# Recurrent stage of a two-block transformer: gates and gelu branch multiplied as plain fp32, statistics' matmuls placed later in three fillers

## The chip, the cores and the metric

The kernel runs on one core of a Trainium2 chip. The metric is the device time of one execution in microseconds (us). The engines are named as in the profile: PE is the matrix engine (PEld its weight loads), DVE the vector engine, ACT the scalar engine, POOL the general-purpose engine, SP the engine whose queue issues the weight transfers.

## What is computed

Two transformer blocks, one after the other, on 256 tokens of 1024 features, all in float32. The first block is, per layer, a gated feed-forward network (FFN), a mixing stage and a second FFN, each followed by a residual and a layer norm; the mixing stage of layer 0 is the recurrent one that the change is about, that of layer 1 is a dilated attention.

```python
def rglru_block(x, w_in, conv_w, conv_b, gate_w, gate_b, lam, w_out):
    y_br, u_br = jnp.split(x @ w_in, 2, axis=-1)          # 1024 -> 2 x 1280
    y = jax.nn.gelu(y_br)
    u = causal_depthwise_conv(u_br, conv_w, conv_b)
    h = rg_lru(u, gate_w, gate_b, lam)
    return (y * h.astype(y.dtype)) @ w_out                # 1280 -> 1024

def rg_lru(u, gate_w, gate_b, lam):
...
    gates = jnp.einsum("bsnc,gncd->gbsnd", ublk, gate_w.astype(jnp.float32)).reshape(2, bsz, s, r)   # 5 blocks of 256 x 256
    gates = gates + gate_b.astype(jnp.float32)[:, None, None, :]
    rec_gate = jax.nn.sigmoid(gates[0])
    in_gate = jax.nn.sigmoid(gates[1])
    log_a = -LRU_C * rec_gate * jax.nn.softplus(-lam.astype(jnp.float32))
    a = jnp.exp(log_a)
    b = jnp.sqrt(-jnp.expm1(2.0 * log_a)) * (in_gate * uf)
...
    _, h = lax.associative_scan(combine, (a, b), axis=1)  # h[t] = a[t] h[t-1] + b[t]
    return h
```

The second block puts 16 more tokens in front (272 in all), norms them, and has two layers of a hybrid mixer and an FFN.

## The kernel before

**Weights.** All weights lie in memory as a stream of 537 units, in the order in which they are used. A unit is eight tiles of 128x128 floats, 512 KB. `_dma` issues the transfer of a unit to one of five `raw` buffers (`RAWS`) on SP's queue. A product of two floats is made of three matmuls of a shorter float format (`F32R`): ACT rounds the weights to `whi` (`_hi`, L88, two casts of 128x512 a unit), DVE subtracts to get the rest `wlo` (`_lo`, L100, two subtractions a unit), and `mm3` multiplies whi by the high part of the data, whi by the low part, wlo by the high part. The data are split in the same way: `gh`, `gl` for a norm's output, `uch`, `ucl` for the convolution's, `yh`, `yl` for the recurrent stage's result, `hh`, `hl` for an FFN's middle. Seven buffers each hold whi and wlo; `pump` keeps them up to six units ahead of use (`LOOK`). With `lo_pool` set, as it is from the end of the recurrent stage's filler to its output projection, `_lo` puts the subtraction on POOL.

**A stage.** `out_proj` ends each stage: per output block of 128 features it sums on PE, then DVE adds the residual (L253), ACT squares (L199), ACT and DVE scale and split the not yet normed data into gh and gl, and running sums of x and of x squared over the blocks go to `acc` (`sums`, L194 and L195, on POOL mostly; the last block's on DVE, L229 and L230). A plain fp32 matmul with a tile of ones (`stats`) adds acc over the partitions and gives the norm's mean and variance. While that is under way, PE does the next stage's `filler`: 32 tiles on the not yet normed data, whose result is corrected afterwards (`fix`). `norm` then writes the normed `xf`, gh and gl. `when` says behind which of the filler's tiles `stats` is called; it is called under a priority raised by 100, and a scheduler sorts each engine's instructions by priority.

**The recurrent stage** (`rg`), from unit 66: filler (4 units), `Pu` (4 units), then, in the order in which PE runs them after the change, gates(0), `Pu2` (units 75 and 76), gates(1), gates(2), gelu(0), gates(3), gelu(1), gates(4), gelu(2), gelu(3), gelu(4). `conv(n)` is eight DVE instructions on a 128x256 half each (L509, L511) that make `uc`, and a split of uc. `gates(n)` is one unit, eight tiles. `gelu(n)` is two units, sixteen tiles on gh and gl, then gelu on ACT and DVE. `root`, `scan` and `close` make the recurrence (the scan is L562) and the split result yh, yl (L160 on ACT, L161 on DVE). out_proj takes units 91 to 100; its first wave sums four output blocks together, k = 0 to 9 in order, half a unit for each k, and needs yh and yl of close(2) at k = 4, of close(4) at k = 8.

Of the kernel before, what the change touches and what calls it, by code (L numbers as in the profile page):

```python
# [8 lines left out]
F32 = mybir.dt.float32  # L9
# [5 lines left out]
SEQ = 256  # L15
# [7 lines left out]
NLN = 11  # L23
LN_EMB = 6
ALPHA = 2.0 ** 0.5
EPS = 1e-5
# [10 lines left out]
KVB = 5  # L37
RAWS = 5
N_HEADS = 16
SLOPES = [2.0 ** (-8.0 * (h + 1) / N_HEADS) for h in range(N_HEADS)]  # L40
# [18 lines left out]
class Builder:  # L59
# [21 lines left out]
    def _hi(self):  # L81
        u = self.nhi
        while self.ndma < min(u + RAWS, N_UNIT):
            self._dma()
        self.nhi += 1
        hi = self.p_w.tile([128, UNIT * 128], F32R, tag="whi", name="whi")
        for q in range(0, UNIT * 128, 512):
            self.nc.scalar.copy(hi[:, q:q + 512], self.raws[u][:, q:q + 512])  # L88
        self.his[u] = hi

    def _lo(self, pool=False):
        u = self.nlo
        while self.nhi <= u:
            self._hi()
        self.nlo += 1
        lo = self.p_w.tile([128, UNIT * 128], F32R, tag="wlo", name="wlo")
        eng = self.nc.gpsimd if pool or self.lo_pool else self.nc.vector
        r, h = self.raws.pop(u), self.his[u].bitcast(F32)
        for q in range(0, UNIT * 128, 512):
            eng.tensor_tensor(lo[:, q:q + 512], r[:, q:q + 512], h[:, q:q + 512], op=ALU.subtract)  # L100
        self.los[u] = lo
# [10 lines left out]
    def w(self, spec, n=1):  # L112
        t = self.used
        u, o = divmod(t, UNIT)
        assert o + n <= UNIT
        if o == 0:
            self.his.pop(u - 1, None)
            self.los.pop(u - 1, None)
            if not self.hold:
                self.pump(2)  # L120
        while self.nlo <= u:
            self._lo()
        self.used += n
        if n == 1:
            self.plan.append(spec)
        else:
            self.plan.extend(spec)
        return self.his[u][:, o * 128:(o + n) * 128], self.los[u][:, o * 128:(o + n) * 128]

# [19 lines left out]

    def mm3(self, out, w, xh, xl, start, stop):  # L150
        self.mm(out, w[0], xh, start, False)
        self.mm(out, w[0], xl, False, False)
        self.mm(out, w[1], xh, False, stop)
# [65 lines left out]
    def prep(self, ms, ln, N, off, fold=True):  # L219
# [14 lines left out]
        for i, m in enumerate(ms):  # L234
            if fold:
                self.fold_hi(m, ln, N, off)
                if i:
                    self.fold_lo(ms[i - 1], ln, N, off)
            self.sums(m, N, off, self.square(m, N, off), nc.vector if ln == 1 else nc.gpsimd)
            if (not fold or ln == LN_EMB - 1) and m:  # L240
                self.scale_in(m - 1, ln, N, off)
# [148 lines left out]
    def group(self, specs, N, kout=False, mid=None):  # L390
# [8 lines left out]
        for i, (k, t) in enumerate(order):  # L399
            if mid and 2 * i == len(order):  # L400
                mid()
            st = k == 0 and (t % 2 == 0 or not shared)
            self.mm3(P[t // 2][:, t % 2, :], self.w(specs[t](k)), self.gh[:, k, 0:N], self.gl[:, k, 0:N], st, k == KD - 1)
        if mid:
# [28 lines left out]

    def ffn(self, sg, su, so, coef, ln_in, ln_out, N, off, eps_in, fold_out=True):
        nc = self.nc
        with self.tc.tile_pool(name="ffn", bufs=1) as p:
# [14 lines left out]
            if ln_in is not None:  # L451
                V = self.filler(specs(0), ln_in, N, off, eps_in, p)
                evac(0, *V)
                j0 = 1
# [6 lines left out]
    def rg(self, ln_in, ln_out, eps):  # L461
        nc = self.nc
        N, off = SEQ, META
        with self.tc.tile_pool(name="rg", bufs=1) as p:
# [37 lines left out]

            uc, uch, ucl = {}, {}, {}

            def conv(n, src):
# [7 lines left out]
                uc[n] = c  # L513
                uch[n] = p.tile([128, 2, N], F32R, tag="uch", name="uch", bufs=2)
                ucl[n] = p.tile([128, 2, N], F32R, tag="ucl", name="ucl", bufs=2)
                nc.vector.tensor_copy(uch[n], c)
                nc.vector.tensor_tensor(ucl[n], c, uch[n].bitcast(F32), op=ALU.subtract)

            def gates(n):
                P = []  # L520
                for g in range(2):
                    b = self.pair_bank(N)
                    for m in range(2):
                        for k in range(2):
                            self.mm3(b[:, m, :], self.w(("rg_gate_w", (0, g, n), k, m * 128)), uch[n][:, k], ucl[n][:, k],
                                     k == 0 and m == 0, k == 1)
                    P.append(b)
# [12 lines left out]
            U = self.filler([wi(10 + c) for c in range(4)], ln_in, N, off, eps, p)  # L540
            self.lo_pool = True
            gy = {}
# [55 lines left out]
            close(4)  # L598
            self.lo_pool = False
            self.out_proj(KR, lambda k: yh[:, k], lambda k: yl[:, k], lambda m, k: ("rg_w_out", (0,), k, m * 128),  # L600
# [650 lines left out]
    def body(self):  # L1251
# [27 lines left out]
        def f2(l):  # L1279
# [11 lines left out]
            lambda: self.attn(3, 4, e1),  # L1291
            lambda: self.ffn(*f1(1, 1), c1, 4, 5, SEQ, META, e1),
            lambda: self.mixer(0, 6, 7, EPS, e1),
            lambda: self.ffn(*f2(0), 0.5 / ALPHA, 7, 8, LTOT, 0, e1),
            lambda: self.mixer(1, 8, 9, e1),
            lambda: self.ffn(*f2(1), 0.5 / ALPHA, 9, 10, SEQ, META, e1, fold_out=False),
        ]
# [152 lines left out]
```

## Time and profile before

| | |
|---|---|
| time, median of 3 runs | 1767.71 us (1766.94 to 1771.07) |
| the profiled execution | 1770.94 us, its span 1769.2 us |
| mean granted clock of PE | 0.979 of full speed |
| busy share of the span | PE 95%, DVE 72%, ACT 58%, POOL 14% |
| waits of PE for other engines in the recurrent stage | some 22 us of about 120 |

The span runs from the first instruction to the last; the time has about 1.7 us around it. In rows of the profile a matmul is listed with its start, and the record of a fp32 matmul stands as two records of the same name. A clock of 1.00 is 2.4 GHz, and the other level is 1.2 GHz, half of it. An idle time in brackets names the instruction whose end released the waiting one.

### The profile page before, as it was taken

To read this page: it belongs to the slowest core of one execution; us is meant where nothing else is said; L and a number is where in the kernel's file an instruction comes from. 1 tells how busy PE (TensorE), PEld (TensorE's weight loads), DVE (VectorE), ACT (ScalarE), POOL (GpSimd) and SP (SyncE) were. 2 spreads that over 40 slices of the span, in tenths; PEclk is the share of its full clock that TensorE was granted. 3 is DMA by queue.
4 is the path that set the end of the run, shared out by engine and by line. 5 is a ranking of instruction groups with operands and counts; after the bars stand their busy time and mean duration, and the time that the engine had idled before them with its cause. 6 is when DMAs were issued, how large, how long until landed. Compare 5 with 4: busy or idle time off the path is not lost.

```text
span 1769.2 us, 34606 instructions
## 1 busy us (share of the span) xinstructions
PE 1687.3 (95%) x13558; PEld 1654.5 (94%) x13558; DVE 1268.4 (72%) x2383; ACT 1031.7 (58%) x2102; POOL 247.8 (14%) x302
## 2 busy tenths in 40 slices
PE   8999978999999999988999999799999999999997
PEld 8999978999999999988899999789999998899996
DVE  6666799966676666588787666987955578696653
ACT  6454666854466544476665455875744466575453
POOL 0001266000010000243220003122000122020001
PEclk9999988999999999989999999899999999999999
DMA  8555433465557655585236555242555545236550
GB/s 293 189 183 188 145 125 133 162 226 189 186 161 280 209 183 187 179 222 152 94 116 217 182 189 197 84 145 95 168 180 179 173 165 170 87 124 227 185 191 25
DMA packets 85597, 299.95 MB, mean 170 GB/s; under 512 B 11372, under 2 KB 13688, under 8 KB 85176
## 3 DMA queue, kind: packets, MB, share of 16 engines
q1 hardware_dynamic: 80216, 283.79, 48.4%
q0 software_dynamic: 2736, 9.48, 1.9%
q10 hardware_dynamic: 2480, 4.46, 0.8%
q8 instruction: 106, 1.74, 0.4%
q14 instruction: 59, 0.48, 0.1%
HBM read 292.34 MB, written 5.24 MB: 168 GB/s over the span
## 4 chain that ended last, share of the span: by engine, by line
PE 78%; DVE 14%; ACT 3%; issue 2%; POOL 1%; DMA 1%; DVEq 0%; SPq 0%; ACTq 0%; POOLq 0%
PE ps L148 78%; DVE wlo L100 3%; ACT whi L88 1%; DMA raw<-in_wst_dram 1%; PE ps L156 1%; DVE q L681 1%; DVE s L700 1%; DVE uc L511 0%; DVE gl L301 0%; DVE xf L253 0%; DVE T L562 0%; POOL wlo L100 0%; DVE nt L292 0%; DVE fv L320 0%; DVE gl L216 0%
## 5 line engine op out<-in xcount | busy, mean ns | idle before, releaser
L100 DVE TENSOR_TENSOR wlo<-raw,whi 128x512 fp32r<-128x512 f32 x1032 | 684.5, 700 | 319.8 <-ACT whi L88 318.1
L88 ACT CAST whi<-raw 128x512 fp32r<-128x512 f32 x1074 | 614.7, 617 | 490.8 <-issue 306.8
L148 PE MATMUL ps<-gh,whi 128*128 128x256 f32 (+3 forms) x2864 | 824.4, 288 | 19.7 <-ACT gh L298 8.4
L148 PE MATMUL ps<-gl,whi 128*128 128x256 f32 (+3 forms) x2864 | 818.9, 286 | 1.1 <-DVE gl L301 1.1
L148 PE MATMUL ps<-gh,wlo 128*128 128x256 f32 (+3 forms) x2864 | 814.6, 284 | 0.0
L148 PEld LDWEIGHTS ps<-gh,whi 128*128 128x128 f32 x2864 | 545.8, 191 | 24.5 <-ACT gh L298 9.1
L148 PEld LDWEIGHTS ps<-gl,whi 128*128 128x128 f32 x2864 | 547.2, 191 | 5.0 <-issue 2.4
L148 PEld LDWEIGHTS ps<-gh,wlo 128*128 128x128 f32 x2864 | 547.2, 191 | 0.5 <-issue 0.2
L148 PE MATMUL ps<-hh,wlo 128*128 128x256 f32 (+1 forms) x1056 | 298.0, 282 | 0.0
L148 PE MATMUL ps<-hh,whi 128*128 128x256 f32 (+1 forms) x1056 | 297.9, 282 | 0.0
L148 PE MATMUL ps<-hl,whi 128*128 128x256 f32 (+1 forms) x1056 | 297.7, 282 | 0.0
L148 PEld LDWEIGHTS ps<-hl,whi 128*128 128x128 f32 x1056 | 199.0, 188 | 0.0
L148 PEld LDWEIGHTS ps<-hh,whi 128*128 128x128 f32 x1056 | 199.0, 188 | 0.0
L148 PEld LDWEIGHTS ps<-hh,wlo 128*128 128x128 f32 x1056 | 198.8, 188 | 0.0
L194 POOL TENSOR_TENSOR acc<-xf 128x256 f32<-128x256 f32 (+1 forms) x10 | 7.6, 760 | 1004.7 <-DVE xf L253 1002.7
L444 DVE TENSOR_TENSOR th<-th,ps 128x512 f32<-128x512 f32 (+1 forms) x62 | 42.9, 691 | 54.5 <-PE ps L148 54.5
L194 POOL TENSOR_TENSOR acc<-acc,xf 128x256 f32<-128x256 f32 (+1 forms) x50 | 45.5, 910 | 192.2 <-DVE xf L253 177.3
L100 POOL TENSOR_TENSOR wlo<-raw,whi 128x512 fp32r<-128x512 f32 x42 | 63.3, 1536 | 46.3 <-ACT whi L88 46.3
L253 DVE SCALAR_TENSOR_TENSOR xf<-ps,xf 128x256 f32<-128x256 f32 (+1 forms) x80 | 32.9, 422 | 41.2 <-PE ps L148 41.0
L199 ACT ACTIVATE sq<-xf 128x256 f32<-128x256 f32 (+1 forms) x88 | 35.6, 410 | 44.6 <-DVE xf L253 36.8
L212 ACT ACTIVATE gh<-xf,prm 128x256 fp32r<-128x256 f32 (+1 forms) x64 | 32.1, 508 | 48.1 <-DVE xf L253 48.1
L216 DVE SCALAR_TENSOR_TENSOR gl<-xf,prm,gh 128x256 fp32r<-128x256 f32 (+1 forms) x64 | 44.4, 705 | 11.1 <-ACT gh L212 11.1
(323 smaller groups left out, 1879.7 us busy)
## 6 DMA issues: line engine op xcount, KB each, us to landing
raw<-in_wst_dram SPq DMA_DIRECT2D x537, 512.0 KB, 3.9
K<-khl POOLq DMA_DIRECT2D x32, 128.0 KB, 6.5
cst<-in_c_mix_dram POOLq DMA_DIRECT2D x2, 1138.0 KB, 5.4
khl<-kh ACTq DMA_DIRECT2D x4, 512.0 KB, 5.9
vsc<-kt ACTq DMA_DIRECT2D x4, 512.0 KB, 5.1
W<-vsc POOLq DMA_DIRECT2D x8, 256.0 KB, 6.0
out_dram<-xf SPq DMA_DIRECT2D x8, 128.0 KB, 1.7
dt<-in_c_dist_dram POOLq DMA_DIRECT2D x1, 576.0 KB, 8.9
```

The costliest lines, as they stand in the source:

```text
L88: self.nc.scalar.copy(hi[:, q:q + 512], self.raws[u][:, q:q + 512])
L100: eng.tensor_tensor(lo[:, q:q + 512], r[:, q:q + 512], h[:, q:q + 512], op=ALU.subtract)
L148: self.nc.tensor.matmul(out, lhsT, rhs, start=start, stop=stop, skip_group_check=True)
L156: self.nc.tensor.matmul(out, in_, self.ident[0:n, 0:n], start=True, stop=True, is_transpose=True, skip_group_check=True)
L194: eng.tensor_tensor(a[:, 0, 0:N], x0, x, op=ALU.add)
L199: self.nc.scalar.activation(sq[:, 0:N], self.xf[:, m, off:off + N], AF.Square)
L212: return self.nc.scalar.activation(self.gh[:, m, c], self.xf[:, m, off:off + N], AF.Copy, scale=g)
L216: return self.nc.vector.scalar_tensor_tensor(self.gl[:, m, c], self.xf[:, m, off:off + N], g, self.gh[:, m, c].bitcast(F32), op0=ALU.mult, ...
L253: self.nc.vector.scalar_tensor_tensor(x, banks[m][:, 0:N], coef, x, op0=ALU.mult, op1=ALU.add)
L444: nc.vector.tensor_tensor(th, th, pu, op=ALU.mult)
L681: nc.vector.scalar_tensor_tensor(Q[pr][e][b, g], src[a], sc, hi.bitcast(F32), op0=ALU.mult, op1=ALU.subtract)
L700: nc.vector.tensor_tensor_reduce(out=s[:, a:z], in0=b[:, a:z], in1=dt[:, a:z], scale=-SLOPES[h], scalar=3e38, op0=ALU.add, op1=ALU.min, ac ...
```

## The change

Four edits. First, the units in `NATIVE`, the five of gates and the ten of gelu, are not split: `_hi` and `_lo` do nothing for them, `w` hands out the raw tile itself, and `mm3` then makes one plain fp32 matmul of it with `uc` or with the normed `xf`; the raw buffer is given back when the next unit is begun. Second, conv no longer splits uc. Third, `lo_pool` is no longer set, so that what is left to split in the stage (units 75, 76 and those of the output projection) is subtracted on DVE. Fourth, for the norms in `SHORT` (4, 7 and 9; norm 1 had both sums on DVE already) the sum of squares goes from POOL to DVE, and three FFNs pass a later `when`.

```diff
+SHORT = (1, 4, 7, 9)
+NATIVE = {74, 77, 78, 81, 84, 79, 80, 82, 83, *range(85, 91)}
...
     def _hi(self):
...
         self.nhi += 1
+        if u in NATIVE:
+            return
         hi = self.p_w.tile([128, UNIT * 128], F32R, tag="whi", name="whi")
...
         self.nlo += 1
+        if u in NATIVE:
+            return
...
         if o == 0:
             self.his.pop(u - 1, None)
             self.los.pop(u - 1, None)
+            if u - 1 in NATIVE:
+                self.raws.pop(u - 1)
...
+        if u in NATIVE:
+            return self.raws[u][:, o * 128:(o + n) * 128], None
...
-    def mm3(self, out, w, xh, xl, start, stop):
+    def mm3(self, out, w, xh, xl, start, stop, x=None):
+        if w[1] is None:
+            self.mm(out, w[0], x, start, stop)
+            return
...
-            self.sums(m, N, off, self.square(m, N, off), nc.vector if ln == 1 else nc.gpsimd)
+            self.sums(m, N, off, self.square(m, N, off), nc.vector if ln == 1 else nc.gpsimd,
+                      nc.vector if ln in SHORT else None)
...
-            self.mm3(P[t // 2][:, t % 2, :], self.w(specs[t](k)), self.gh[:, k, 0:N], self.gl[:, k, 0:N], st, k == KD - 1)
+            self.mm3(P[t // 2][:, t % 2, :], self.w(specs[t](k)), self.gh[:, k, 0:N], self.gl[:, k, 0:N], st, k == KD - 1,
+                     self.xf[:, k, LTOT - N:])
...
                 uc[n] = c
-                uch[n] = p.tile([128, 2, N], F32R, tag="uch", name="uch", bufs=2)
-                ucl[n] = p.tile([128, 2, N], F32R, tag="ucl", name="ucl", bufs=2)
-                nc.vector.tensor_copy(uch[n], c)
-                nc.vector.tensor_tensor(ucl[n], c, uch[n].bitcast(F32), op=ALU.subtract)
...
-                            self.mm3(b[:, m, :], self.w(("rg_gate_w", (0, g, n), k, m * 128)), uch[n][:, k], ucl[n][:, k],
-                                     k == 0 and m == 0, k == 1)
+                            self.mm3(b[:, m, :], self.w(("rg_gate_w", (0, g, n), k, m * 128)), None, None,
+                                     k == 0 and m == 0, k == 1, uc[n][:, k])
...
-            self.lo_pool = True
...
-            self.lo_pool = False
...
-            lambda: self.ffn(*f1(1, 1), c1, 4, 5, SEQ, META, e1),
+            lambda: self.ffn(*f1(1, 1), c1, 4, 5, SEQ, META, e1, when=(2, 2)),
...
-            lambda: self.ffn(*f2(0), 0.5 / ALPHA, 7, 8, LTOT, 0, e1),
+            lambda: self.ffn(*f2(0), 0.5 / ALPHA, 7, 8, LTOT, 0, e1, when=(2, 0)),
...
-            lambda: self.ffn(*f2(1), 0.5 / ALPHA, 9, 10, SEQ, META, e1, fold_out=False),
+            lambda: self.ffn(*f2(1), 0.5 / ALPHA, 9, 10, SEQ, META, e1, fold_out=False, when=(2, 2)),
```

How instructions stand on PE around the first gates, before (L148 is the line that issues every matmul; x2 counts equal neighbours):

```order
L148 MATMUL ps<-gh,whi 128x256
L148 MATMUL ps<-uch,whi 128x256 x2
L148 MATMUL ps<-gl,whi 128x256
L148 MATMUL ps<-gh,wlo 128x256
L148 MATMUL ps<-gh,whi 128x256
L148 MATMUL ps<-gl,whi 128x256
L148 MATMUL ps<-gh,wlo 128x256
L148 MATMUL ps<-gh,whi 128x256
L148 MATMUL ps<-ucl,whi 128x256
```

and after the change (where that line is L158):

```order
L158 MATMUL ps<-gh,whi 128x256
L158 MATMUL ps<-gl,whi 128x256
L158 MATMUL ps<-gh,wlo 128x256
L158 MATMUL ps<-uc,raw 128x256 x8
L158 MATMUL ps<-gh,whi 128x256
L158 MATMUL ps<-gl,whi 128x256
```

Before, the first two matmuls of gates(0) stood among Pu2's, with 16 of Pu2's ahead of them; now gates(0) is eight plain matmuls between Pu and Pu2. Behind it stand Pu2's 48, then 16 on uc, 16 on xf, 8, 16, 8 and 48, and the output projection.

On ACT at the end of the recurrent stage, after the change (L92 casts the weights to whi, L557 and L560 are gelu's square and tanh, L173 is close's cast to yh):

```order
L173 CAST yh<-gy 128x512
L92 CAST whi<-raw 128x512
L557 ACTIVATE gy<-ps 128x512
L92 CAST whi<-raw 128x512 x2
L560 ACTIVATE gy<-gy 128x512
L92 CAST whi<-raw 128x512 x4
L173 CAST yh<-gy 128x512
L557 ACTIVATE gy<-ps 128x512
L92 CAST whi<-raw 128x512 x4
L560 ACTIVATE gy<-gy 128x512
L92 CAST whi<-raw 128x512 x4
L173 CAST yh<-gy 128x512
```

The first row is close(2), the last close(4). Three more casts stand just ahead of the first row, and none stands between the first gates and these. So 18 casts, the whole of units 91 to 99, now stand ahead of close(4)'s yh.

On PE at the filler behind norm 7 (N = 272, one of the three with a later `when`), before:

```order
L148 MATMUL ps<-hh,wlo 128x272
L148 MATMUL ps<-gh,whi 128x274
L148 MATMUL ps<-gl,whi 128x274
L148 MATMUL ps<-gh,wlo 128x274
L148 MATMUL ps<-gh,whi 128x274
L148 MATMUL ps<-gl,whi 128x274
L148 MATMUL ps<-gh,wlo 128x274
L148 MATMUL ps<-gh,whi 128x274
L148 MATMUL ps<-gl,whi 128x274
L148 MATMUL ps<-gh,wlo 128x274
L148 MATMUL ps<-acc,ones 128x272 x2
L148 MATMUL ps<-gh,whi 128x274
```

and after:

```order
L158 MATMUL ps<-hh,wlo 128x272
L158 MATMUL ps<-gh,whi 128x274
L158 MATMUL ps<-gl,whi 128x274
L158 MATMUL ps<-gh,wlo 128x274
L158 MATMUL ps<-gh,whi 128x274
L158 MATMUL ps<-gl,whi 128x274
L158 MATMUL ps<-gh,wlo 128x274
L158 MATMUL ps<-gh,whi 128x274
L158 MATMUL ps<-gl,whi 128x274
L158 MATMUL ps<-gh,wlo 128x274
L158 MATMUL ps<-acc,ones 128x272 x2
L158 MATMUL ps<-gh,whi 128x274
```

The statistics' matmuls (acc,ones) stand behind nine of the filler's matmuls, before and after; behind norms 4 and 9 they stand behind twelve, before and after. On PE nothing but the recurrent stage's rows differs.

## Rows read from the trace of the kernel before

**Rows 1.** The page's busy times: us (share of the span) xinstructions.

```profile
PE 1687.3 (95%) x13558; PEld 1654.5 (94%) x13558; DVE 1268.4 (72%) x2383; ACT 1031.7 (58%) x2102; POOL 247.8 (14%) x302
```

**Rows 2.** Windows of the recurrent stage: busy us of PE, PEld, DVE, ACT, POOL, PEclk, DMA.

```profile
209.50:226.50 17.00, 14.07 (x113) 13.45 (x112) 17.00 (x36) 10.87 (x27) 10.59 (x7) 1.00 0.37 125
226.50:241.80 15.30, 6.40 (x32) 6.23 (x31) 15.29 (x29) 4.95 (x13) 5.25 (x4) 0.67 0.33 103
241.80:287.10 45.30, 43.25 (x364) 43.07 (x364) 39.79 (x54) 37.98 (x72) 32.64 (x22) 1.00 0.34 117
287.10:306.70 19.60, 12.56 (x79) 11.88 (x78) 18.90 (x22) 12.16 (x23) 12.62 (x8) 0.74 0.42 145
306.70:329.50 22.80, 21.61 (x178) 21.00 (x178) 22.61 (x50) 15.48 (x34) 0.00 (x0) 1.00 0.63 211
```

**Rows 3.** Waits of PE from 196 to 330 us: total, times, longest.

```profile
PE ps L148 <- DVE uch L516: 8.9, 1, 8.9
PE ps L148 <- DVE yl L161: 7.7, 2, 6.9
PE ps L148 <- ACT gh L298: 2.2, 1, 2.2
PE ps L148 <- DVE uc L511: 2.0, 1, 2.0
```

**Rows 4.** Timeline of PE at the first gates: start, us, what [idle before].

```profile
226.46 0.28 PE L148 MATMUL ps<-gh,whi 128*128 128x256 f32 x1
235.64 0.77 PE L148 MATMUL ps<-uch,whi 128*128 128x256 f32 x2 [8.90 <-DVE uch L516]
```

**Rows 5.** Timeline of PE in the output projection's first wave.

```profile
300.74 0.58 PE L148 MATMUL ps<-yl,whi 128*128 128x256 f32 x1 [6.89 <-DVE yl L161]
...
301.34 0.41 PE L148 MATMUL ps<-yh,whi 128*128 128x256 f32 x1
301.55 0.41 PE L148 MATMUL ps<-yl,whi 128*128 128x256 f32 x1
...
306.77 0.28 PE L148 MATMUL ps<-yl,whi 128*128 128x256 f32 x1
306.89 0.28 PE L148 MATMUL ps<-yh,wlo 128*128 128x256 f32 x1
```

**Rows 6.** Timeline of POOL from 206 to 233 us, first and last of five rows.

```profile
207.31 3.05 POOL L100 TENSOR_TENSOR wlo<-raw,whi 128x512 fp32r<-128x512 f32 x2 [15.02 <-ACT whi L88]
...
230.05 2.53 POOL L100 TENSOR_TENSOR wlo<-raw,whi 128x512 fp32r<-128x512 f32 x2 [0.22 <-ACT whi L88]
```

**Rows 7.** A group of DVE, 287.1 to 301.5 us: xcount | busy, mean ns | idle.

```profile
L161 DVE TENSOR_TENSOR yl<-gy,yh 128x512 fp32r<-128x512 f32 x1 | 1.7, 1681 | 0.0
```

**Rows 8.** The same group from 302 to 313.7 us.

```profile
L161 DVE TENSOR_TENSOR yl<-gy,yh 128x512 fp32r<-128x512 f32 x2 | 1.4, 684 | 0.0
```

**Rows 9.** Timeline of PE at the last norm: two plain fp32 matmuls.

```profile
1755.14 0.59 PE L148 MATMUL ps<-xf,ones 128*128 128x256 f32 x2
1755.57 0.59 PE L148 MATMUL ps<-sq,ones 128*128 128x256 f32 x2
```

**Rows 10.** DMA issues from 200 to 330 us: xcount, KB each, median us to landing.

```profile
raw<-in_wst_dram SPq DMA_DIRECT2D x35, 512.0 KB, 3.3
```

**Rows 11.** Timeline of all engines at norm 4's statistics.

```profile
908.05 1.28 ACT L283 ACT_TABLE_LOAD   x1
908.18 0.75 POOL L195 TENSOR_TENSOR acc<-acc,sq 128x256 f32<-128x256 f32 x1
...
909.46 0.40 ACT L199 ACTIVATE sq<-xf 128x256 f32<-128x256 f32 x1
...
909.96 0.43 DVE L230 TENSOR_TENSOR acc<-acc,sq 128x256 f32<-128x256 f32 x1 [0.75 <-ACT sq L199]
...
910.44 0.92 PE L148 MATMUL ps<-acc,ones 128*128 128x512 f32 x1 [2.67 <-DVE acc L230]
```

**Rows 12.** The page's costliest groups, ACT's cast of weights.

```profile
L88 ACT CAST whi<-raw 128x512 fp32r<-128x512 f32 x1074 | 614.7, 617 | 490.8 <-issue 306.8
```

More of the change, by code (lines that the diff above doesn't have):

```diff
@@ L431, in out_proj, with ffn @@
                 self.pump(AHEAD)
-    def ffn(self, sg, su, so, coef, ln_in, ln_out, N, off, eps_in, fold_out=True):
+    def ffn(self, sg, su, so, coef, ln_in, ln_out, N, off, eps_in, fold_out=True, when=(1, 3)):
         nc = self.nc
@@ L451, in ffn @@
             if ln_in is not None:
-                V = self.filler(specs(0), ln_in, N, off, eps_in, p)
+                V = self.filler(specs(0), ln_in, N, off, eps_in, p, when=when)
                 evac(0, *V)
@@ L501, in wi @@
                 return lambda k: ("rg_w_in", (0,), k, c * 128)
-            uc, uch, ucl = {}, {}, {}
+            uc = {}
             def conv(n, src):
```

## The prediction

> **What bounds the kernel now.** I read the page first. PE is busy 95% of the span [rows 1], and where PE is busy a second more of its work is a second more of time. So the question is where the missing 5% lies, and whether the change works there. The list of PE's waits between 196 and 330 us, the recurrent stage, holds 20.8 us in its four longest kinds [rows 3], and the windows of this stage show what surrounds them [rows 2]. From the last matmul of the stage's filler (209.5 us) to the statistics of the next norm (329.5 us) it takes 120 us. In the first two windows DVE is busy for 17.00 of 17.00 and 15.29 of 15.30 us: the chain runs through DVE, and PE waits for it, 8.9 us ahead of the first gates [rows 4] and 6.89 us in the output projection's first wave [rows 5].
>
> Two things make these waits dearer than they look. First, PE's granted clock is 0.67 and 0.74 in the windows that hold them, and 1.00 elsewhere [rows 2]. With two levels, 1.00 and 0.50, this is (1 - 0.67) x 2 x 15.3 = 10.1 us and (1 - 0.74) x 2 x 19.6 = 10.2 us at half clock, part of it while PE stands. PE restarts at 235.64 and at 300.74 [rows 4, 5] and gets its full clock near 241.8 and 306.6: from then on matmuls start 0.12 us apart, before that 0.21 [rows 5]. So it does some 6.2 + 5.9 us of work at half speed, and half of that, 6.0 us, is lost. Second, the DVE is not slow by its own work. The same subtraction into yl takes 1681 ns at 299 us and 684 ns after 302 us [rows 7, 8]. POOL works on wlo in the first case (8 instructions in that window) and not at all in the second (0 in the last window) [rows 2]. A DVE instruction with a POOL subtraction beside it takes 1.0 us longer, as if it waited for it.
>
> **The change part by part.**
>
> *Plain fp32 tiles.* The gates are 40 tiles and gelu 80. A split tile is three matmuls 0.119 us apart (0.12 in [rows 5]), 0.356 us. For a plain one the nearest row is the last norm's: two fp32 matmuls of 256 columns, each with two records and two weight loads, start 0.43 us apart [rows 9]. PE gets 120 x (0.43 - 0.356) = 8.9 us more work. If the second weight load were free and the rate that of one split matmul for each record, a tile would cost 0.24 and PE would save 14 us; the row says otherwise, and I take 0.43.
>
> This is the point on which a rule speaks against the change. The Trainium skill, page "FP8 and Floating Point Precision", section "TensorE Precision Notes", says that true fp32 takes four passes through the array. Three passes become four: as an estimate from it and the 0.119 us, 0.475 a tile and 14.3 us in all, 5.4 more than by the row, which would make the gain below 9 instead of 14.5. No native tile with fresh weights stands in the rows shown, and I keep the row's 0.43.
>
> *POOL no longer subtracts.* POOL's first subtraction in the stage starts at 207.31 and the last two ahead of the first gates at 230.05; the five rows hold 12 [rows 6]. One of them is itself held up, so I count 11.5 us by which they push the DVE chain. The norm's first gh comes earlier too, and of the 2.2 us that PE waits for it [rows 3] I leave 0.8. Pu's 32 tiles then end at 209.5 + 0.8 + 11.4 = 221.7. The first gates, which start at 235.64 now, have their uc at 235.6 - 11.5 = 224.1 (the dropped split of uc may give some tenths more). The wait of 8.9 becomes 2.4.
>
> From there PE has 120 plain tiles (51.6) and Pu2's 16 split ones (5.7): 57.3 us, to 281.4. Behind the gates nothing should wait: the DVE work of this part is covered by PE's, since 45.3 us of it now hold 39.8 of DVE with 22 POOL subtractions [rows 2], which blocked it by about as many us. What moves to DVE, 14 subtractions of 0.68 us of units 75, 76 and 91 to 95, is hidden under the gelu tiles; without that cover it would cost 9.5 us, and that is no more than the blocking that goes.
>
> *The raw buffers are held by PE.* With five buffers the transfer of unit u + 5 now waits until PE has done unit u. Inside gelu that is four units of 3.4 us ahead against 3.3 us from issue to landing [rows 10]: no wait. At the end it bites. Unit 95 can only be issued when unit 90 is done, at 281.4, and lands at 284.7. Units 96 to 99 follow, each some 2.0 us later: the last window moves 211 GB/s with the DMA engines busy 0.63 of the time [rows 2], so a unit takes 2.5 us at that rate and 1.6 with the engines full, and I take the middle. ACT's order puts the casts of all these units ahead of close(4)'s yh (the second fence on the change). So yh waits for unit 99 (292.7), two casts of 0.62 [rows 12] and its own, then yl 0.68: 295.2. PE reaches k = 8, where it needs them, at 281.4 + 32 x 0.356 = 292.8. A wait of 2.4 us takes the place of the 6.89; from 0, if the units land at 1.6 us each, to 7.6, if each takes the 3.3 of [rows 10]. I add 1.0 for the clock: half of the two us or so that a wait of this length could put at 1.2 GHz. Then 48 tiles (17.1) and the four tiles that stand ahead of the statistics (1.4).
>
> *Sum.* 295.2 + 17.1 + 1.0 + 1.4 = 314.7 instead of 329.5: 14.8 us less. As a check from the other side: 252 split tiles are 89.7 us of work, and 120 - 89.7 = 30.3 us are waits, half clock and small gaps. Of these go 30.3 - 8.9 (new work) - 0.8 - 2.4 - 2.4 - 1.0 = 14.8.
>
> *Squares on DVE, and the later statistics.* On PE nothing moves: behind norm 7 the statistics stand behind nine filler matmuls before and after, behind norms 4 and 9 behind twelve. The later `when` costs and gains nothing there. The sum of squares leaves POOL, but POOL is not what the statistics wait for. At norm 4 POOL's last sum starts at 908.18 and takes 0.75; the square of the last block starts only at 909.46, as ACT loads a table from 908.05 on for 1.28 us, and the last sum on DVE (909.96) and PE (910.44) follow it [rows 11]. What is late stays late. If I were wrong, each of the three places could give back at most its wait, 2.67 us here, or lose the 0.43 of one sum put ahead of the residual; I take 0.
>
> The span of this execution is 1769.2 and its time 1770.94, which is 3.2 above the median of the runs, 1767.71. The gain does not hang on that, so the forecast is 1767.7 - 14.5 = 1753.2, with 0.3 of the 14.8 left to the three norms' places.
>
> **The rivals.** *The held buffers cost more (15%).* If the units land 3.3 us apart, the wait in the output projection is 7.6 us and PE's clock drops as it does now, some 2.9 us; with 3 us more ahead of the first gates the gain is 14.8 - 5.2 - 1.9 - 3.0 = 4.7, about 1763; with the first part alone, 1760. For it: ACT's order shows 18 casts in a row of few other instructions. Against it: the rate of [rows 2] in a stretch where several transfers are queued.
>
> *PE is the bound and DVE's lateness stays (6%), slower.* If the DVE chain was late by something other than POOL (ACT's links in it, the raw data), the 8.9 and 6.89 us stay, PE's work grows by 8.9 and the time is 1776.6. It decides where the waits and the half clock together shrink by less than 8.9 of the 27. This is also what the skill's rule on four passes says for a kernel whose PE is busy 95%. Against it stand 1681 and 684 ns for the same instruction [rows 7, 8].
>
> *Both in part (6%)*, so that the new work eats what the waits give: within 0.3% of now, 1762.5 to 1773. *The edit of the statistics does what it says (in the forecast's range)*: up to 3 x 2.67 = 8.0 more off, which the order on PE and the table load speak against.
>
> **How the numbers follow.** The forecast case, a gain of 9 to 21, has 73%. Its best end is no new wait at all: 30.3 - 8.9 = 21.4, so 1746. The first rival reaches to 1763 and has its middle at 1760; a range up to 1761 leaves out part of it and the others, below 2 in 10 together. About 0.3% (5.3 us) is what a measurement of this kernel can tell from no change. Faster by more has the forecast, most of the first rival: 0.87; the same 0.07; slower 0.06.
>
> **What would show it.** Right: PE's plain records start 0.215 us apart; POOL has no wlo; DVE's yl takes 0.68 each time; gates(0) starts near 224 and the output projection near 281; the next statistics near 315; a wait of some us for yh or yl of close(4) with ACT held at a cast for a raw landing; the waits at norms 4, 7 and 9 within 0.5 us of now. Wrong: plain tiles above 0.55 us (14.8 more over 120 tiles, 0.12 each, and the gain is gone), PE waiting for raw inside gelu, or DVE instructions of 1.5 us with POOL idle.

## The result, and the profile after

The changed kernel takes 1741.47 us (median of 4 runs, 1738.82 to 1742.37), the kernel before 1767.33 in the same comparison. The ratio is 0.9851, 95% interval 0.9839 to 0.9864: 26.3 us less, 24.0 to 28.5. The forecast was 14.5 less, at best 21.4, so the time lies below its range of 1746 to 1761. The sign was right, and most of the gain lies in the stage where the forecast had it; the size was not right, and the three norms gave some 6 us where it had nothing.

The page of the kernel after, its busy times, beside [rows 1]:

```profile
PE 1680.6 (97%) x13438; PEld 1645.4 (95%) x13438; DVE 1240.6 (71%) x2403; ACT 1017.2 (59%) x2072; POOL 168.6 (10%) x242
```

The same stage of the kernel after in windows (end of the filler to the first gates; gates(0) to gelu(0); the rest of gates and gelu; the output projection's first 32 tiles, up to where it needs close(4); to the next statistics), with the columns of [rows 2]:

```profile
209.00:220.90 11.90, 11.65 (x97) 11.43 (x97) 11.90 (x38) 8.30 (x22) 0.00 (x0) 1.00 0.01 2
220.90:244.00 23.10, 23.10 (x132) 21.03 (x131) 19.68 (x43) 13.25 (x26) 0.00 (x0) 1.00 0.40 137
244.00:278.30 34.30, 34.30 (x162) 30.20 (x160) 26.51 (x45) 22.78 (x39) 0.00 (x0) 1.00 0.54 180
278.30:289.70 11.40, 11.40 (x97) 11.37 (x96) 10.23 (x18) 8.72 (x16) 0.00 (x0) 1.00 0.90 296
289.70:308.40 18.70, 18.70 (x159) 18.57 (x157) 18.01 (x43) 13.06 (x29) 0.00 (x0) 1.00 0.65 218
```

POOL has nothing to do here, and PE is busy for 99.15 of 99.4 us at full clock throughout. In the list of PE's waits this stage has no row left, where [rows 3] had four. The two waits of [rows 4, 5] are gone completely. The timeline of PE at the first gates and at the start of the output projection, where no row has an idle time behind it:

```profile
220.87 0.28 PE L158 MATMUL ps<-gh,wlo 128*128 128x256 f32 x1
220.99 1.24 PE L158 MATMUL ps<-uc,raw 128*128 128x256 f32 x5
...
277.40 1.24 PE L158 MATMUL ps<-xf,raw 128*128 128x256 f32 x5
278.29 0.47 PE L158 MATMUL ps<-yh,whi 128*128 128x256 f32 x1
```

DVE's instructions that feed uc (the split of the normed data, and the correction of the filler's result), before and after, by group from the filler's end to some us behind the start of the first gates (before 209.5 to 241.8 us, after 209.0 to 224.2):

```profile
L301 DVE TENSOR_TENSOR gl<-xf,gh 128x256 fp32r<-128x256 f32 x8 | 5.9, 747 | 0.0
L320 DVE SCALAR_TENSOR_TENSOR fv<-nm,sc,fv 128x256 f32<-128x256 f32 x4 | 4.8, 1242 | 0.0
```

```profile
L315 DVE TENSOR_TENSOR gl<-xf,gh 128x256 fp32r<-128x256 f32 x8 | 3.4, 419 | 0.0
L334 DVE SCALAR_TENSOR_TENSOR fv<-nm,sc,fv 128x256 f32<-128x256 f32 x4 | 1.8, 479 | 0.0
```

The same instructions on the same shapes: 747 ns become 419, 1242 become 479. Close's yl takes 683 to 693 ns each time now, as in [rows 8] and not as in [rows 7].

The whole stage, from statistics to statistics, is one row for each kernel (before, then after):

```profile
199.45:329.50 130.05, 107.94 (x835) 105.01 (x834) 123.32 (x211) 89.42 (x178) 63.29 (x42) 0.92 0.42 140
```

```profile
198.95:308.46 109.51, 109.26 (x715) 101.99 (x713) 96.13 (x213) 75.25 (x148) 0.00 (x0) 1.00 0.51 168
```

That is 20.5 us less. The rest of the 26.3 lies at norms 4, 7 and 9, where the forecast had nothing.

### The profile page after: what moved, and what is told of

Same layout as the page of the kernel before. It is cut to its first block, busy times and chain, and to the rows that moved or that the text cites. A ratio compares the mean times of both kernels' runs of the same rounds, so it can differ in the third digit from the quotient of the medians.

```text
span 1737.0 us, 34255 instructions
## 1 busy us (share of the span) xinstructions
PE 1680.6 (97%) x13438; PEld 1645.4 (95%) x13438; DVE 1240.6 (71%) x2403; ACT 1017.2 (59%) x2072; POOL 168.6 (10%) x242
## 4 chain that ended last, share of the span: by engine, by line
PE 83%; DVE 12%; ACT 2%; issue 2%; DMA 1%; POOL 0%; DVEq 0%; SPq 0%; ACTq 0%
PE ps L158 82%; DVE wlo L106 3%; DVE q L690 1%; DMA raw<-in_wst_dram 1%; PE ps L169 1%; DVE gl L229 1%; DVE s L709 1%; DVE xf L267 1%; ACT whi L92 0%; DVE acc L208 0%; DVE nt L306 0%; DVE nt L307 0%; DVE rstd L292 0%; DVE cp L870 0%; DVE gl L315 0%
## 5 line engine op out<-in xcount | busy, mean ns | idle before, releaser
L92 ACT CAST whi<-raw 128x512 fp32r<-128x512 f32 x1044 | 598.5, 617 | 491.4 <-issue 306.9
L158 PE MATMUL ps<-gh,whi 128*128 128x256 f32 (+4 forms) x2784 | 799.5, 287 | 14.8 <-ACT whi L92 6.9
L158 PE MATMUL ps<-gl,whi 128*128 128x256 f32 (+4 forms) x2784 | 794.3, 285 | 0.5 <-DVE gl L315 0.4
L158 PE MATMUL ps<-gh,wlo 128*128 128x256 f32 (+4 forms) x2784 | 790.3, 284 | 0.0
L158 PEld LDWEIGHTS ps<-gh,whi 128*128 128x128 f32 x2784 | 528.6, 190 | 19.1 <-ACT whi L92 8.3
L158 PEld LDWEIGHTS ps<-gl,whi 128*128 128x128 f32 x2784 | 530.1, 190 | 3.3 <-issue 1.8
L158 PEld LDWEIGHTS ps<-gh,wlo 128*128 128x128 f32 x2784 | 530.2, 190 | 0.4 <-issue 0.2
L158 PE MATMUL ps<-hh,wlo 128*128 128x256 f32 (+1 forms) x1056 | 298.0, 282 | 0.0
L158 PE MATMUL ps<-hh,whi 128*128 128x256 f32 (+1 forms) x1056 | 298.0, 282 | 0.0
L158 PE MATMUL ps<-hl,whi 128*128 128x256 f32 (+1 forms) x1056 | 297.7, 282 | 0.0
L158 PEld LDWEIGHTS ps<-hl,whi 128*128 128x128 f32 x1056 | 199.0, 188 | 0.0
L158 PEld LDWEIGHTS ps<-hh,whi 128*128 128x128 f32 x1056 | 199.0, 188 | 0.0
L158 PEld LDWEIGHTS ps<-hh,wlo 128*128 128x128 f32 x1056 | 198.9, 188 | 0.0
L229 DVE SCALAR_TENSOR_TENSOR gl<-xf,prm,gh 128x256 fp32r<-128x256 f32 (+1 forms) x64 | 40.3, 638 | 11.1 <-ACT gh L225 11.1
L309 ACT ACTIVATE xf<-nt,prm 128x256 f32<-128x256 f32 (+1 forms) x72 | 42.6, 604 | 7.8 <-DVE nt L307 7.7
```

Source lines behind the costliest of these rows:

```text
L158: self.nc.tensor.matmul(out, lhsT, rhs, start=start, stop=stop, skip_group_check=True)
L229: return self.nc.vector.scalar_tensor_tensor(self.gl[:, m, c], self.xf[:, m, off:off + N], g, self.gh[:, m, c].bitcast(F32), op0=ALU.mult, ...
L309: nc.scalar.activation(self.xf[:, i, off:off + N], t, AF.Identity, scale=g, bias=b)
```

## The experiments

In all of them the lengths of the stage are those between the two statistics, as in the last two rows.

**1. The squares alone, and `when` alone.**

```diff
             self.sums(m, N, off, self.square(m, N, off), nc.vector if ln == 1 else nc.gpsimd,
+                      nc.vector if ln in SHORT else None)
```

> The kernel before, with only the sums of squares of norms 4, 7 and 9 moved from POOL to DVE. Theory A (a POOL sum holds up the DVE instruction beside it, so the last blocks' residual, square and sum all come sooner): PE's waits ahead of the three statistics fall from 2.67, 1.76 and 2.75 us to about 1.5, 1.0 and 1.6, as in the changed kernel, and the stretches of 3.4 us at half clock behind them go too: 3.1 us from the waits and up to 5.1 from the clock, in all 3 to 8 us less, about 1762. Rival (the forecast's own: the table load on ACT sets the last square, whatever POOL does): no change, 1767 within 2 us, and waits within 0.3 us of before.

Measured: 1762.2 us, ratio 0.9964 (0.9952 to 0.9977), by it 6.4 us less (4.1 to 8.5). This is theory A. The timeline of this kernel at norm 4, all engines (L217 is gl, L196 and L231 the sums of squares, L255 the residual, L200 the square, L285 the table load):

```profile
900.39 0.41 DVE L196 TENSOR_TENSOR acc<-acc,sq 128x256 f32<-128x256 f32 x1
...
900.73 0.47 DVE L217 SCALAR_TENSOR_TENSOR gl<-xf,prm,gh 128x256 fp32r<-128x256 f32 x1
...
901.73 0.41 DVE L255 SCALAR_TENSOR_TENSOR xf<-ps,xf 128x256 f32<-128x256 f32 x1
...
902.20 0.29 PE L149 MATMUL ps<-gh,whi 128*128 128x258 f32 x1
...
903.00 1.28 ACT L285 ACT_TABLE_LOAD   x1
...
904.41 0.40 ACT L200 ACTIVATE sq<-xf 128x256 f32<-128x256 f32 x1
...
905.32 1.12 PE L149 MATMUL ps<-acc,ones 128*128 128x512 f32 x2 [1.51 <-DVE acc L231]
```

and the rows of the kernel before that answer to the first three, on POOL and DVE, with the first filler matmul:

```profile
905.39 1.18 POOL L195 TENSOR_TENSOR acc<-acc,sq 128x256 f32<-128x256 f32 x1
...
905.90 0.95 DVE L216 SCALAR_TENSOR_TENSOR gl<-xf,prm,gh 128x256 fp32r<-128x256 f32 x1
...
906.16 0.29 PE L148 MATMUL ps<-gh,whi 128*128 128x258 f32 x1
...
906.77 0.41 DVE L253 SCALAR_TENSOR_TENSOR xf<-ps,xf 128x256 f32<-128x256 f32 x1
```

Counted from the filler's first matmul, the residual of block 6 came 0.61 us after it before and 0.47 ahead of it now: DVE's gl stood still beside POOL's sum (0.95 instead of 0.47 us), and the blocks ahead of it have the same pairs. From the first wave's residuals to that of block 6 DVE takes 11.81 us (889.92 to 901.73) and took 12.89 (893.88 to 906.77), although it now makes the sums of squares itself. The table load follows the square of that block, so it starts 0.80 us after the filler's begin and not 1.89 ([rows 11], 908.05 - 906.16); what follows it moves along, and PE waits 1.51 us, not 2.67. The load is in the chain, as the forecast had it, but it is not where the chain begins.

By the traces the larger part of it is the clock. PE's stretch at half clock behind the wait is gone as well. Windows of 7.5 us from just ahead of norm 4's statistics, of the kernel before and of this one:

```profile
909.90:917.40 7.50, 6.96 (x39) 6.03 (x40) 6.11 (x10) 5.66 (x12) 0.00 (x0) 0.77 0.43 141
```

```profile
904.70:912.20 7.50, 6.88 (x52) 6.40 (x53) 7.34 (x14) 6.83 (x14) 0.00 (x0) 1.00 0.40 138
```

52 matmuls start in it instead of 39; 13 at 0.12 us are 1.6 us. The stretches from the statistics of norms 4, 7 and 9 to the next ones are 1.57, 1.61 and 1.52 us shorter, 4.7 together. With waits that are 1.16, 0.79 and 1.13 us shorter, the three places give 3.1 + 4.7 = 7.8 us by the traces, and the runs give 6.4. The stretch that ends at norm 4 is shorter by 4.6 us in this trace, of which the wait is 1.16; the rest is not counted here, since the stretch took 152.8 to 157.5 us in executions of kernels that all have this edit.

The later `when` was not run alone, as it moves nothing: outside of the recurrent stage the changed kernel, which has it, and this one, which has not, run the same instructions in the same order on PE, DVE, ACT and POOL. So the title's statistics "placed later" are not later in fact, and what the norms give is the squares.

**2. The recurrent stage alone.** The changed kernel without `SHORT` and `when`:

```diff
-SHORT = (1, 4, 7, 9)
...
-                      nc.vector if ln in SHORT else None)
```

> The changed kernel without the edit of the statistics: only the recurrent stage differs from the kernel before. If the parts are independent, the stage keeps its 20.5 us (from the statistics ahead of it to those behind it 109.5 us instead of 130.1) and the time is about 1746.8; what the changed kernel is below it (about 5 us) is the sums of squares. If the stage had also given the later norms a better clock, the time would be nearer to 1742, and the first run's gain nearer to 0.

Measured: 1746.29 us, ratio 0.9881 (0.9865 to 0.9896), 21.0 us less, as expected. The stage takes 109.52 us; its window row:

```profile
199.79:309.31 109.52, 109.28 (x716) 101.99 (x714) 96.04 (x213) 75.31 (x148) 0.00 (x0) 1.00 0.49 168
```

The parts add up: 21.0 + 6.4 = 27.4 against 26.3, with 2 to 3 us of uncertainty on each.

**3. POOL's subtractions to DVE, everything still split.** The kernel before with one line taken out:

```diff
-            self.lo_pool = True
```

> The kernel before, with only the setting taken out that puts the stage's 42 subtractions of weights on POOL: they go to DVE at about 0.69 us each, all products stay split. Theory A (each POOL subtraction costs DVE about 1.05 us of standing still, 44 us in all, more than the 29 us that it takes off DVE): DVE's need in the stage falls from 114 to about 99 us, PE's waits ahead of the first gates and in the output projection shrink to some 5 us together, and the time falls by 8 to 18 us, to about 1754. Rival (DVE is late by its own load, POOL takes work off it): 29 us more on an engine that was busy all the time at both waits, so 5 to 20 us slower than before, 1773 to 1787. That POOL's help is neutral: 1767.

Measured: 1755.78 us, ratio 0.9934 (0.992 to 0.9948), 11.7 us less. This is theory A. Work was put on the engine that PE waits for, and the kernel got faster. The stage takes 118.92 us:

```profile
199.12:318.04 118.92, 106.97 (x843) 104.30 (x841) 115.99 (x252) 90.18 (x179) 0.00 (x0) 0.96 0.44 147
```

DVE has 41 instructions more than before and is busy 7.3 us less (123.32 there). What is left on DVE is real work, and PE still waits for it, more than the 5 us expected; the longest of PE's waits in this stage:

```profile
PE ps L148 <- DVE uch L516: 6.0, 2, 4.3
PE ps L148 <- ACT whi L88: 2.6, 1, 2.6
PE ps L148 <- DVE ucl L517: 1.1, 2, 0.6
```

So of the stage's 20.5 us the removal of POOL gives 11.1, and the plain fp32 format (with the split of uc that it makes needless) the other 9.4, although it puts about 9 us more work on PE: it takes splits off DVE and ACT. These shares hold for this order of the two edits. With the format first, experiment 4, the format gives 16.5 (130.05 to 113.58) and the removal of POOL 4.1, because the format itself takes 28 of the 42 subtractions from POOL.

**4. POOL back, beside plain fp32 gates and gelu.**

```diff
+            self.lo_pool = True
             gy = {}
...
+            self.lo_pool = False
             self.out_proj(KR, lambda k: yh[:, k], lambda k: yl[:, k], lambda m, k: ("rg_w_out", (0,), k, m * 128),
```

> The changed kernel with POOL given back the subtractions of what is still split in the stage, those of units 75, 76 and 91 to 99: 22 of 1.3 to 2.6 us. Theory A (POOL holds DVE up): DVE instructions of 1.4 to 1.5 us come back beside each of them, the low halves of units 91 to 99 come late (18 subtractions of 1.5 us are 27 us on POOL, between the first cast at 268 us and their use from 278 to 290), and PE waits in the output projection: 4 to 12 us slower than the changed kernel, 1746 to 1753. Rival (what mattered was that DVE lost the splits of the gates' and gelu's units, not where the rest runs): within 2 us of the changed kernel.

Measured: 1744.52 us, ratio 0.9873 (0.9852 to 0.9894); by the trace the stage takes 113.58 us, 4.1 more than in the changed kernel. That is at the low end of theory A, and the intervals of the two ratios overlap, so it rests on the traces. Only 14 subtractions land on POOL, not the 22 I had counted; by their number and order they are those of units 75, 76 and 91 to 95:

```profile
L106 POOL TENSOR_TENSOR wlo<-raw,whi 128x512 fp32r<-128x512 f32 x14 | 20.7, 1507 | 75.4 <-ACT whi L92 75.4
```

PE's waits in the stage, which are all of the 4.1 but 0.3:

```profile
PE ps L158 <- ACT gh L312: 1.7, 1, 1.7
PE ps L158 <- DVE gl L315: 1.3, 1, 1.3
PE ps L158 <- DVE yl L174: 0.8, 1, 0.8
```

So the place was not the expected one: only the last 0.8 us lie in the output projection. The first two come from three subtractions at 206.72 us, ahead of `Pu`. DVE's timeline beside them, three of its instructions on 128x10 elements:

```profile
206.68 0.16 DVE L506 TENSOR_SCALAR e<-z 128x10 f32<-128x10 f32 x1
...
207.09 1.25 DVE L508 SCALAR_TENSOR_TENSOR e<-e,z 128x10 f32<-128x10 f32 x1
...
211.59 0.16 DVE L508 SCALAR_TENSOR_TENSOR e<-e,z 128x10 f32<-128x10 f32 x1
```

An instruction on ten columns takes 1.25 us beside POOL and 0.16 without it. It isn't slowed in proportion to its size, it waits. The Trainium skill, page "SBUF — State Buffer", section "Who interferes with whom", has this rule: a DVE instruction with two inputs in SBUF contends with a GpSimd instruction that reads SBUF, because its second input comes through the read interface that the two engines share. These rows agree with it. One row of the kernel before, beside POOL's subtraction of [rows 6] at 230.05 us, shows that an instruction with a single tensor as input (and columns of parameters) can be held too, for 1.43 us where its like takes 0.40:

```profile
230.04 1.43 DVE L509 TENSOR_SCALAR uc<-fv,prm 128x256 f32<-128x256 f32 x1
```

**5. Raw buffers in turn.**

```diff
-        raw = self.p_raw.tile([128, UNIT * 128], F32, tag="raw", name="raw")
+        raw = self.p_raw.tile([128, UNIT * 128], F32, tag=f"raw{u % RAWS}", name="raw", bufs=1)
```

> The changed kernel with the five raw buffers used strictly in turn, unit u + 5 in the buffer of unit u, which is what the forecast assumed. In the changed kernel a split unit's buffer comes back as soon as its low part is subtracted, so that unit 95 is issued at 274.2 us and unit 99 at 279.5. In turn, unit 95 has to wait until PE is done with unit 90, at 278.3, and 96 to 99 stand behind it in the queue; at the 1.7 us a unit of that stretch (296 GB/s) unit 99 lands at about 288.3 and close(4)'s low part is ready at 290.9, for a product due at 289.7: PE waits some 1.2 us and the time is 1 to 2.5 us above the changed kernel. By the forecast's own price (2 us a unit) the wait is 2.4 us, with the clock 3.4 in all. Rival (buffers play no part): the same within 1 us and no wait there.

Measured: 1743.64 us, ratio 0.9872 (0.9851 to 0.9893); the stage takes 112.17 us, 2.7 more than in the changed kernel. The size is near the expected one, the place is not, so the size is chance. PE does not wait for close(4); the low part is ready at 290.5 us and due at 290.6. It waits at the next statistics:

```profile
312.02 1.55 PE L158 MATMUL ps<-acc,ones 128*128 128x512 f32 x2 [2.63 <-DVE acc L243]
```

The casts come late, DVE has nine subtractions in a row behind them (290.43 to 295.93), and the residuals and sums of the next norm queue up behind those. The edit also changed the order on SP's queue, where later units' transfers now stand ahead of earlier ones, so it doesn't isolate the buffers; that a held buffer costs some us here is supported, not shown.

**6. Less plain fp32.** PE is the bound of the stage now, and a split tile is 0.075 us cheaper on it. Five kernels ask how many tiles can go back to the split form, with the subtractions on DVE; the third is the changed kernel itself, for comparison.

```diff
-NATIVE = {74, 77, 78, 81, 84, 79, 80, 82, 83, *range(85, 91)}
+NATIVE = {74, 77, 78, 81, 84}
```

> The changed kernel with only the five units of gates as plain fp32; the ten of gelu are split again, with the subtraction on DVE. By the trace of the changed kernel PE waits for nothing in the stage, so its work sets the end: 80 tiles at 0.356 instead of 0.432 us are 6.0 us less. DVE gets 20 subtractions of 0.69 us, 13.8 us, where it stands still for some 12.4 us of the 68.8 between the first gates and the second half of the output projection's first wave. If DVE can take them: 4 to 6 us less than the changed kernel, about 1736. If DVE becomes the bound, a wait ahead of close(4)'s product brings it back: 1741 to 1746. The plain format itself would be what the gain needs only if this run came out near the kernel before.

```diff
+NATIVE = {74, 77, 78, 81, 84, *range(87, 91)}
```

> The changed kernel with the gates' units and the last four of gelu's (87 to 90) as plain fp32, the first six of gelu's split, with the subtraction on DVE. PE's work falls by 48 tiles of 0.075 us, 3.6 us; DVE gets 12 subtractions, 8.3 us, in a stretch where it stands still for 12.4. If PE's work alone sets the end of the stage: 3 to 4 us less than the changed kernel, about 1738. If DVE is already too full, none of it comes, or a wait of PE for uc or for a low part returns: 1741 to 1745.

The changed kernel, unaltered:

> The changed kernel once more, unaltered, beside the next two on one chip. 1741.5 within 2 us, and no wait of PE for another engine between the statistics at 199 us and those at 308; the stretch between them takes 109.5 us. If the undisturbed stage was luck of one execution, a wait of a us or more shows there.

```diff
+NATIVE = {74, 77, 78, 81, 84, 79, 80, 82, 83}
```

> The changed kernel with the gates' units and the first four of gelu's (79, 80, 82, 83) as plain fp32, the last six split with the subtraction on DVE: the other half of gelu than in the run with the tail as plain fp32, where PE waited 1.8 us for uc, because DVE had the subtractions of the first units to do beside the convolutions. PE's work falls by 48 tiles of 0.075 us, 3.6 us; the 12 subtractions, 8.3 us, now lie in the stretch from 244 to 278 us where DVE stands still for 7.8. If it is as the traces say: no wait for uc, a wait of at most 1 us in the output projection, 2 to 4 us less than the changed kernel, about 1738.5. Rival (DVE full at the end of the stage, then the low parts of units 91 to 99 are late): within 1 us of the changed kernel, or slower.

```diff
+NATIVE = {74, 77, 78, 81, 84, 79, 80}
```

> The changed kernel with the gates' units and the first two of gelu's (79 and 80) as plain fp32, the last eight split on DVE. PE's work falls by 64 tiles, 4.8 us; DVE gets 16 subtractions, 11.0 us, for the 12.4 that it has. If the wait for uc goes and the one at the statistics (1.4 us with all of gelu split) stays: some 3.5 us less than the changed kernel, 1738. If DVE is too full for the last units: a wait of 1 to 4 us in the output projection or at the statistics, and 1739 to 1743.

| plain fp32 | tiles split again | time, us | ratio to before | stage, us | PE's waits in it, us |
|---|---|---|---|---|---|
| gates, gelu (the change, again) | 0 | 1740.21 | 0.9845 (0.9826 to 0.9865) | 109.51 | none |
| gates, last 4 units of gelu | 48 | 1737.76 | 0.9839 (0.9820 to 0.9858) | 109.85 | 1.8, 0.2, 0.2 |
| gates, first 4 units of gelu | 48 | 1740.65 | 0.9847 (0.9829 to 0.9865) | 109.09 | 1.4, 0.8, 0.3 |
| gates, first 2 units of gelu | 64 | 1740.66 | 0.9843 (0.9825 to 0.9861) | 111.16 | 2.1, 0.8 |
| gates | 80 | 1740.38 | 0.9844 (0.9830 to 0.9857) | 107.92 | 1.4, 1.3, 0.8 |

The changed kernel came out as before, 109.51 us and no wait, so the undisturbed stage was not the luck of one execution. No mixture can be told from it by the time. With the last four units plain the time is the one that was expected if PE's work set the end, but the trace is not: the wait for uc is back, and the stage is 0.3 us longer than the changed kernel's. With the first four plain there is no wait for uc, as expected, but others came; with the first two plain PE waits 2.9 us in the output projection, the second of the two cases expected. The work that PE saves (3.6 to 6.0 us) comes back as waits for DVE or ACT, and in the second and fourth row of the table as half clock behind such a wait; where it is most, PE saves 6.0 and the stage 1.6, of the 4 to 6 expected. The row of the stage with only the gates as plain fp32, and PE's waits in it:

```profile
198.85:306.77 107.92, 104.19 (x798) 100.30 (x796) 106.70 (x233) 84.83 (x168) 0.00 (x0) 1.00 0.50 167
```

```profile
PE ps L158 <- DVE acc L243: 1.4, 1, 1.4
PE ps L158 <- DVE uc L526: 1.3, 1, 1.3
PE ps L158 <- DVE yl L174: 0.8, 1, 0.8
```

DVE is busy for 106.70 of 107.92 us. The changed kernel stands close to where the two engines balance, and near there the split of gelu's units between the formats matters little: for them the plain format is worth nothing measurable, once POOL is off. What it is worth lies with the gates. From the kernel of experiment 3, where all is split (118.92 us), to the one with only the gates plain (107.92 us) the stage gets 11.0 us shorter, more than the 9.4 that the format gives in the whole change. Two edits make this step, the gates' five units and the dropped split of uc; no run parts them.

## Why the prediction was wrong

**The main mechanism was right.** POOL's subtractions made DVE's instructions wait, DVE's lateness made PE wait, and PE's waits cost it the clock. Experiment 3 shows it without any change of format: 11.1 us of the stage, and its granted clock goes from 0.92 to 0.96. The rival "PE is the bound and DVE's lateness stays" fell by the same run. "Both in part" and "the held buffers cost more" did not happen.

**Plain fp32 tiles: right.** The plain records start 0.2158 us apart, 0.432 a tile; 0.43 was taken. From the first gates to the output projection it is 278.29 - 220.99 = 57.3 us, and 57.3 was the forecast. The Trainium skill's rule of four passes (page "FP8 and Floating Point Precision", section "TensorE Precision Notes"), priced with the 0.119 us of a split matmul, gave 0.475 and was too dear. The Trainium skill's page "TensorE: Matmul & The Clock Gate", section "Step-by-step: what each phase is for", has one column entering per cycle; by that four passes of 256 columns at 2.4 GHz are an estimated 0.427 us. The measured 0.432 agrees with that estimate; by it the price of a pass was wrong and not the four.

**POOL no longer subtracts: the size was off.** I moved uc forward by 11.5 us and left PE 2.4 us of waiting for the first gates, and 0.8 for gh. PE starts the gates at 220.99 with no wait, so uc came at least 14.1 us sooner, counted from the same point of the stage (the filler of this execution ended 0.5 earlier), and the 2.4 and the 0.8 did not come. DVE's instructions ahead of the gates were held for 12.0 us in all, summed over the twelve between 207 and 235 us that are longer than their like, by 0.50 to 1.10 each. The cast of uch (0.42) and a weight subtraction of a unit that is plain now (0.68) have gone out of the same queue; about one us I can't name. So of the 2.6 us that the forecast missed here 0.5 is the count of POOL's instructions, 1.1 is work that left the queue with the format (the forecast named only some tenths, and left them out of the sum), and 1.0 stays open.

**The raw buffers are held by PE: this step failed.** It had unit u + 5 wait for PE's end of unit u, and so unit 95 issued when PE is done with gelu, and a wait of 2.4 us with 1.0 of clock. PE was done with gelu at 278.3 us, and unit 95 was issued 4.1 us ahead of that; the row of its transfer on SP's queue:

```profile
274.19 0.33 SPq L80 DMA_DIRECT2D raw<-in_wst_dram  x1
```

The longest of SP's waits between 262 and 285 us:

```profile
SPq L80 <- DVE wlo L106: 9.9, 6, 2.2
SPq L80 <- PE ps L158: 7.3, 4, 3.0
```

The buffers are not used in turn: the next transfer takes the one that comes back first. From unit 91 on units are split, and give their buffer back as soon as DVE has the low part; 93, 95, 97 and 98 went to such a buffer, and only 94, 96 and 99 to one that PE gave back. The price was too high as well: with 296 GB/s from 278.3 to 289.7 us a unit takes 1.8 us, not 2.0. So the last casts ahead of close(4) were done at 287.4 us, 9.1 behind PE's end of gelu, where the forecast had them done 12.5 behind it (unit 99's landing at 292.7, two casts, gelu's end at 281.4). The rows of ACT and of DVE that end it (the last casts and close(4)'s yh, and its yl):

```profile
285.00 2.44 ACT L92 CAST whi<-raw 128x512 fp32r<-128x512 f32 x4 [1.22 <-DMA raw<-in_wst_dram]
287.34 0.61 ACT L173 CAST yh<-gy 128x512 fp32r<-128x512 f32 x1
```

```profile
287.98 0.69 DVE L174 TENSOR_TENSOR yl<-gy,yh 128x512 fp32r<-128x512 f32 x1 [0.67 <-ACT yh L173]
```

yl is ready at 288.7 and due at 278.3 + 32 x 0.356 = 289.7. A wait of 2.4 us, 3.4 with the clock, was forecast where 1.0 us was to spare. In experiment 5, 0.1 us was to spare. The lower bound of 0 for this wait does not follow from the forecast's own terms: with 1.6 us a unit they give yl at 293.6, 0.8 behind the 292.8.

The forecast kept 2.4 + 0.8 + 2.4 + 1.0 = 6.6 us of waits and half clock, of which none came. What is left is 0.9 us of gaps (99.5 us from the filler's end, for 98.6 of work), and so the stage's gain is 30.3 - 8.9 - 0.9 = 20.5.

**Squares on DVE: this step failed.** "What is late stays late", a term of 0, stopped at the table load without asking what its own start hung on. It hung on the residual of block 6, behind a DVE instruction with POOL's sum beside it, the same thing that the forecast saw in the stage a few lines above. It gave 6.4 us instead of 0. The bound of 8.0 was worked out and not put into the sum, and that 6.4 lies near it is luck: it counted the three waits whole and no clock, where 3.1 came from the waits and up to 4.7 from the clock. That the `when` moves nothing was right.

So 14.5 became 26.3: 5.7 us more in the stage (20.5 for 14.8), the rest at the three norms, for which the forecast had taken 0.3 off.

## What to carry to other kernels

Before a helper engine is given work, look at the rows of the engine that it is meant to relieve: if the same instruction has two lengths, and the long one stands beside the helper's, the help can cost more than it saves. Here 0.69 us on DVE was cheaper than 1.5 us on POOL, which held DVE for 0.5 to 1.1 us at a time. Follow a late chain back past the longest link to its first late row, and price a held buffer by who gives it back, one by one. Once no wait was left here, moving work between two engines that were both nearly full gave nothing that could be measured.

## What the runs showed of the hardware

The length of a DVE instruction beside POOL's does not follow its size: ten columns took 1.25 us instead of 0.16. A wait of PE can cost more than itself: behind 2.67 us at norm 4 the granted clock was 0.77 over 7.5 us, so PE was at 1.2 GHz for part of them, and 13 matmuls fewer started than behind 1.51 us at the same place in experiment 1, where it stayed at 1.00. And the stretch between the statistics of norms 3 and 4, with the same code in both, took 152.8 us in one execution of the changed kernel and 157.0 in one of the mixtures of experiment 6, at a granted clock of 0.98 and 0.95. Single executions therefore differ by some us outside of the edit, and lengths of a stage were compared here rather than spans.
